# Loading x two batches per transfer, and moving the uneven share of the DMA engines from the first load to the first store

## Chip, cores, metric

One NeuronCore of a Trainium2 chip. The metric is the time of one execution on the device in microseconds (us). A kernel's time is the median of its runs; the profile is of one execution, and its span (first to last instruction) is about 1.8 us shorter than the time of the same run. PE is the TensorE matmul engine, DVE the VectorE, ACT the ScalarE; PSUM is the memory that PE writes its results to. The "pool queue" holds the transfers that GpSimd issues. A "packet" is one contiguous piece that one DMA engine moves.

## The reference

```python
x:      (32, 512, 1024) float32
weight: (32, 1024, 768) float32
np.matmul(x, weight).astype(np.float32)     # (32, 512, 768)
```

Each batch reads 2 MB of x and 3 MB of weight and writes 1.5 MB. There is no reuse between batches, so 32 batches have to move about 208 MiB.

## The kernel before

Loads go through the pool queue, which casts to bf16 on the way. PE transposes x (two bf16 as one float32 word), DVE copies the transposed words out of PSUM, PE multiplies, ACT and DVE move the result to `out_sb`, and the pool queue stores it. Near the end, stores are held back and sent by the sync engine.

```python
x_pool = ctx.enter_context(tc.tile_pool(name="x", bufs=5))     # w 4, xT 8, out 7
x_view = x.rearrange("b (mi mo) k -> b mi mo k", mi=P)         # partition mi: 4 rows, 16 KB
def load_x(b):
    xs[b] = x_pool.tile([P, MT, K], BF16, name="x_sb")
    nc.gpsimd.dma_start(out=xs[b], in_=x_view[b])
def transpose(b, mt):
    pt = tpsum.tile([P, JT, P], F32, name="pt")
    pairs = xs[b].bitcast(F32)
    for j in range(JT):
        nc.tensor.transpose(pt[:, j, :], pairs[:, mt, j::JT], ident)
    xT = xT_pool.tile([P, JT, P, 2], BF16, name="xT")
    nc.vector.tensor_copy(...)                                  # contiguous
    return xT
# ... first x: three quarters in one transfer, the last quarter in 18 small ones
nc.sync.dma_start(x_first[:, :MT - 1], x_view[0, :, :MT - 1])
at = 0
for few, times in ((4, 2), (5, 1), (6, 1)):
    for _ in range(times):
        for first in range(at, at + 4):
            rows = slice(first, at + 4 * few, 4)
            nc.sync.dma_start(x_first[rows, MT - 1], x_view[0, rows, MT - 1])
        at += 4 * few
# ... (two more)
for b in range(B):
    if b + AHEAD + 1 < B: load_x(b + AHEAD + 1)                 # AHEAD = 3
    if b + AHEAD < B:     load_w(b + AHEAD)
    # ... store of batch b - 1 on the pool queue, then the batch's compute
```

The Trainium skill (DMA: Bandwidth & Descriptors, "Why a DMA increments its semaphore by 16 and not by 1") says that the number of engines of a transfer is the largest one up to 16 that divides the outermost sizes of both its sides (here the partitions), and that the sync engine's transfers take the lowest-numbered. By that, a transfer over 4, 5 or 6 partitions does not use all 16 DMA engines, and the small transfers make a skew: more bytes for engines 0 to 3, fewer for the rest. The trace's packets carry no engine number.

Of the kernel before, what the change touches and what calls it, by code (L numbers as in the profile page):

```python
# [8 lines left out]
F32 = mybir.dt.float32  # L9
BF16 = mybir.dt.bfloat16  # L10


@with_exitstack
def kernel(
    ctx: ExitStack,
    tc: tile.TileContext,
    x: bass.AP,
    weight: bass.AP,
    out: bass.AP,
):  # L20
    nc = tc.nc
    B, M, K = x.shape
    _, _, N = weight.shape
    P = 128
    MT = M // P
    KT = K // P
    JT = KT // 2
    N2 = 2 * N
    CHUNKED = {B - 4: (4, 4), B - 3: (4, 4), B - 2: (4, 4), B - 1: (4, 2, 2)}
    AHEAD = 3  # L30
    LATE = 4
    HELD = 3

    const = ctx.enter_context(tc.tile_pool(name="const", bufs=1))
    first_pool = ctx.enter_context(tc.tile_pool(name="first", bufs=1))
    w_pool = ctx.enter_context(tc.tile_pool(name="w", bufs=4))
    x_pool = ctx.enter_context(tc.tile_pool(name="x", bufs=5))
    xT_pool = ctx.enter_context(tc.tile_pool(name="xT", bufs=8))
    out_pool = ctx.enter_context(tc.tile_pool(name="out", bufs=7))
    tpsum = ctx.enter_context(tc.tile_pool(name="tpsum", bufs=2, space=bass.MemoryType.PSUM))  # L40
    mpsum = ctx.enter_context(tc.tile_pool(name="mpsum", bufs=2, space=bass.MemoryType.PSUM))



    w_view = weight.rearrange("b (ki ko) n -> b ki ko n", ki=P)
    x_view = x.rearrange("b (mi mo) k -> b mi mo k", mi=P)
    out_view = out.rearrange("b (mi mo) n -> b mi (mo n)", mi=P)

    xs, ws, outs = {}, {}, {}

    def banks():
        return [mpsum.tile([P, 512], F32, name=f"pm{i}") for i in range(3)]

    def load_x(b):
        xs[b] = x_pool.tile([P, MT, K], BF16, name="x_sb")
        nc.gpsimd.dma_start(out=xs[b], in_=x_view[b])  # L56

    def load_w(b):
        ws[b] = w_pool.tile([P, KT, N], BF16, name="w_sb")
        at = 0  # L60
        for n in CHUNKED.get(b, (KT,)):
            nc.gpsimd.dma_start(out=ws[b][:, at:at + n, :], in_=w_view[b, :, at:at + n, :])  # L62
            at += n

    def transpose(b, mt):

        pt = tpsum.tile([P, JT, P], F32, name="pt")
        pairs = xs[b].bitcast(F32)
        for j in range(JT):
            nc.tensor.transpose(pt[:, j, :], pairs[:, mt, j::JT], ident)  # L70
        xT = xT_pool.tile([P, JT, P, 2], BF16, name="xT")
        nc.vector.tensor_copy(  # L72
            xT.rearrange("p j m r -> p (j m r)"), pt.bitcast(BF16).rearrange("p j m -> p (j m)")
        )
        return xT

    def transpose_first(mt):

        xT = xT_pool.tile([P, JT, P, 2], BF16, name="xT")
        for h in range(2):  # L80
            pt = tpsum.tile([P, JT, P], F32, name="pt")
            for i in range(JT):
                nc.tensor.transpose(pt[:, i, :], x_first[:, mt, JT * h + i::KT], ident)  # L83
            nc.vector.tensor_copy(  # L84
                xT[:, 2 * h:2 * h + 2].rearrange("p j m r -> p j r m"),
                pt.rearrange("p (j r) m -> p j r m", r=2),
            )
        return xT



    SPLITS = (
        ((0, 0, 0, 512), (1, 0, 512, N - 512)),
        ((1, N - 512, 0, 1024 - N), (2, 0, 1024 - N, N2 - 1024)),
    )

    def matmuls(pm, half, xT, b, kos, together):
        for ko in kos:
            for i, (bank, at, off, size) in enumerate(SPLITS[half]):
                shares = half == 1 and i == 0  # L100
                nc.tensor.matmul(  # L101
                    pm[bank][:, at:at + size],
                    xT[:, ko // 2, :, ko % 2],
                    ws[b][:, ko, off:off + size],
                    start=(ko == 0 and not (together and shares)),
                    stop=(ko == KT - 1),
                    skip_group_check=together,
                )

    def evacuate(b, pair, pm):  # L110
        o = outs[b][:, pair * N2:(pair + 1) * N2]
        nc.scalar.copy(o[:, 0:512], pm[0])  # L112
        nc.vector.tensor_copy(o[:, 512:1024], pm[1])  # L113
        nc.scalar.copy(o[:, 1024:N2], pm[2])  # L114

    with tc.manual_schedule():
        x_first = first_pool.tile([P, MT, K], F32)

        nc.sync.dma_start(x_first[:, :MT - 1], x_view[0, :, :MT - 1])
        at = 0  # L120
        for few, times in ((4, 2), (5, 1), (6, 1)):
            for _ in range(times):
                for first in range(at, at + 4):
                    rows = slice(first, at + 4 * few, 4)
                    nc.sync.dma_start(x_first[rows, MT - 1], x_view[0, rows, MT - 1])
                at += 4 * few
        for rows in (slice(at, 80), slice(80, P)):
            nc.sync.dma_start(x_first[rows, MT - 1], x_view[0, rows, MT - 1])
        load_w(0)
        ident = const.tile([P, P], F32)  # L130
        make_identity(nc, ident)
        for b in range(1, AHEAD):
            load_x(b)
            load_w(b)
        load_x(AHEAD)

        pending = []
        for b in range(B):
            if b + AHEAD + 1 < B:
                load_x(b + AHEAD + 1)  # L140
            if b + AHEAD < B:
                load_w(b + AHEAD)
            if b <= B - LATE:
                if b > 0:
                    pending.append(b - 1)
                if b + AHEAD < B - HELD or b == B - LATE:
                    for at in pending:
                        nc.gpsimd.dma_start(out=out_view[at], in_=outs[at])  # L148
                    pending = []
            if b == B - 1:  # L150
                halves = [slice(pair * N2, (pair + 1) * N2) for pair in range(2)]
                nc.sync.dma_start(out_view[b - 1, :, halves[0]], outs[b - 1][:, halves[0]])
                for late in range(B - LATE, B - 2):
                    nc.sync.dma_start(out_view[late], outs[late])
                nc.sync.dma_start(out_view[b - 1, :, halves[1]], outs[b - 1][:, halves[1]])
            outs[b] = out_pool.tile([P, MT * N], F32, name="out_sb")
            if b not in CHUNKED:
                turn = transpose if b else lambda _, mt: transpose_first(mt)
                xT = {mt: turn(b, mt) for mt in (0, 1)}
                for pair in range(2):  # L160
                    pm = banks()
                    for half in range(2):
                        if pair == 0:
                            matmuls(pm, half, xT[half], b, range(KT), False)
                            xT[2 + half] = turn(b, 2 + half)
                        else:
                            matmuls(pm, half, xT[2 + half], b, range(KT), False)
                    evacuate(b, pair, pm)
                continue
            xT = {0: transpose(b, 0)}  # L170
            pms = [banks() for _ in range(2)]
            at = 0
            for n in CHUNKED[b]:
                last = at + n == KT
                for mt in range(MT):
                    if mt + 1 not in xT and mt + 1 < MT:
                        xT[mt + 1] = transpose(b, mt + 1)
                    matmuls(pms[mt // 2], mt % 2, xT[mt], b, range(at, at + n), True)
                    if last and mt % 2 == 1:
                        pair = mt // 2  # L180
                        evacuate(b, pair, pms[pair])
                        if b == B - 1:
                            nc.sync.dma_start(out_view[b, :, halves[pair]], outs[b][:, halves[pair]])
                at += n
# [30 lines left out]
```

## Time and profile before

516.93 us, the median of the runs of the first measurement. The run that left the profile took 517.03.

From the page of the kernel before: the busy time of each engine, then rows of the 40 slices (each digit is tenths of a slice busy), then the DMA queues with packets, MB and share of 16 engines' span, and the traffic with HBM.

```profile
PE 419.6 (81%) x2576; PEld 275.7 (54%) x2576; DVE 129.8 (25%) x196; ACT 76.2 (15%) x129; POOL 51.7 (10%) x102
...
PE   0039999999999988798978879977898978989980
...
DMA  8999999999999999999999999999999999999996
...
q0 software_dynamic: 13824, 126.88, 96.7%
q1 hardware_dynamic: 1232, 8.39, 4.1%
...
HBM read 167.77 MB, written 50.33 MB: 423 GB/s over the span
```

The DMA row is 9 in every slice but the first and the last. PE is idle for its first two slices. From the same page, two groups (line, operation, output and input, count, then busy us and mean ns of one, then idle time before them and what ended it), and what the chain that ended last is made of:

```profile
L101 PE MATMUL pm<-w_sb,xT 128*128 128x256 bf16 (+1 forms) x2048 | 364.7, 336 | 47.9 <-DMA w_sb<-in_weight_dram 44.0
L72 DVE COPY xT<-pt 128x1024 bf16<-128x1024 bf16 x124 | 82.8, 689 | 203.0 <-PE pt L70 203.0
...
DMA 69%; PE 25%; DVE 2%; issue 1%; ACT 0%; POOLq 0%
```

The chain's pieces at its start and its end (start us, length us, what):

```profile
0.74 9.28 DMA x_first<-in_x_dram
...
10.04 10.89 DMA x_first<-in_x_dram
...
20.95 12.60 DMA x_first<-in_x_dram
...
33.64 3.89 PE pt L83 x16
...
501.22 0.58 ACT out_sb L114
```

The first x needs three rounds of transfers and PE starts at 33.6 us. It catches up by 127 us, and from then on waits for w. The pool queue's issues in the steady part, from the timeline, show the pace of one batch (198.85 - 183.03 us here, 15.8 us):

```profile
183.03 0.53 POOL L56 DMA_DIRECT2D x_sb<-in_x_dram  x1 [6.65 <-DMA w_sb<-in_weight_dram]
186.72 0.53 POOL L62 DMA_DIRECT2D w_sb<-in_weight_dram  x1 [3.16 <-DMA out_dram<-out_sb]
191.63 0.54 POOL L148 DMA_DIRECT2D out_dram<-out_sb  x1 [4.38 <-DVE xT L72]
198.85 0.53 POOL L56 DMA_DIRECT2D x_sb<-in_x_dram  x1 [6.69 <-DMA w_sb<-in_weight_dram]
```

### The profile page before, as it was taken

Reading aid. Unit: us, or ns where it says so; the run is one execution under the profiler, and the core shown is the slowest. Engines: PE = TensorE matmul, PEld = TensorE weight load, DVE = VectorE, ACT = ScalarE, POOL = GpSimd, SP = SyncE. Lnnn points to the kernel's source line nnn. Section 1 sums busy time; section 2 is a strip of 40 time slices with the busy share of each in tenths; the row PEclk is TensorE's granted clock in tenths of the full one; section 3 lists DMA queues with packets and bytes.
Section 4 is the critical chain, followed back from the end, with each engine's and each line's share of the span. In section 5 each row is a group of like instructions: output and inputs, shape, how many; then the busy total and the mean of one; then the engine's idle time right before and its main releaser. Section 6 shows DMA issues by size and latency. Waiting matters only on the chain.

```text
span 515.2 us, 6001 instructions
## 1 busy us (share of the span) xinstructions
PE 419.6 (81%) x2576; PEld 275.7 (54%) x2576; DVE 129.8 (25%) x196; ACT 76.2 (15%) x129; POOL 51.7 (10%) x102
## 2 busy tenths in 40 slices
PE   0039999999999988798978879977898978989980
PEld 0026666666666655465645545654564645656650
DVE  0023333333333313133122231322331313332320
ACT  0001111111111101011111111110110111111110
POOL 3000111111000110100101001100111010111000
PEclk9999999999999989799988997998997989999995
DMA  8999999999999999999999999999999999999996
GB/s 233 223 225 220 209 278 277 260 238 276 274 276 267 237 269 276 275 272 245 254 276 275 276 254 243 273 278 275 266 239 265 276 276 274 240 253 213 291 430 272
DMA packets 15081, 135.64 MB, mean 263 GB/s; under 512 B 1744, under 2 KB 1744, under 8 KB 3536
## 3 DMA queue, kind: packets, MB, share of 16 engines
q0 software_dynamic: 13824, 126.88, 96.7%
q1 hardware_dynamic: 1232, 8.39, 4.1%
q8 instruction: 20, 0.33, 0.2%
q14 instruction: 5, 0.04, 0.0%
HBM read 167.77 MB, written 50.33 MB: 423 GB/s over the span
## 4 chain that ended last, share of the span: by engine, by line
DMA 69%; PE 25%; DVE 2%; issue 1%; ACT 0%; POOLq 0%
DMA w_sb<-in_weight_dram 31%; PE pm L101 22%; DMA out_dram<-out_sb 16%; DMA x_sb<-in_x_dram 15%; DMA x_first<-in_x_dram 6%; PE pt L70 2%; PE pt L83 1%; DVE out_sb L113 1%; DVE xT L72 1%; ACT out_sb L112 0%; ACT out_sb L114 0%; POOLq L62 0%; POOLq L148 0%; POOLq L56 0%
## 5 line engine op out<-in xcount | busy, mean ns | idle before, releaser
L101 PE MATMUL pm<-w_sb,xT 128*128 128x256 bf16 (+1 forms) x2048 | 364.7, 336 | 47.9 <-DMA w_sb<-in_weight_dram 44.0
L101 PEld LDWEIGHTS <-xT 128*128 128x128 bf16 x2048 | 203.3, 100 | 184.6 <-issue 50.5
L72 DVE COPY xT<-pt 128x1024 bf16<-128x1024 bf16 x124 | 82.8, 689 | 203.0 <-PE pt L70 203.0
L112 ACT COPY out_sb<-pm 128x512 f32<-128x512 f32 x64 | 37.5, 585 | 286.7 <-PE pm L101 286.7
L70 PEld LDWEIGHTS pt<-ident,x_sb 128*128 128x128 f32 x496 | 72.9, 206 | 6.3 <-issue 1.3
L113 DVE COPY out_sb<-pm 128x512 f32<-128x512 f32 x64 | 44.0, 687 | 128.1 <-PE pm L101 128.1
L70 PE MATMUL pt<-ident,x_sb 128*128 128x128 f32 x496 | 75.4, 286 | 0.0
L114 ACT COPY out_sb<-pm 128x512 f32<-128x512 f32 x64 | 37.5, 586 | 138.2 <-PE pm L101 138.0
L62 POOL DMA_DIRECT2D w_sb<-in_weight_dram x37 | 19.8, 534 | 154.9 <-PE pm L101 74.6
L56 POOL DMA_DIRECT2D x_sb<-in_x_dram x31 | 16.5, 532 | 173.4 <-DMA w_sb<-in_weight_dram 129.4
L83 PE MATMUL pt<-ident,x_first 128*128 128x128 f32 x32 | 6.0, 350 | 33.6 <-DMA x_first<-in_x_dram 33.6
L148 POOL DMA_DIRECT2D out_dram<-out_sb x28 | 15.0, 536 | 93.2 <-DMA x_sb<-in_x_dram 55.9
L83 PEld LDWEIGHTS pt<-ident,x_first 128*128 128x128 f32 x32 | 5.0, 204 | 34.3 <-issue 33.6
L84 DVE CAST xT<-pt 128x512 bf16<-128x512 f32 x8 | 5.6, 726 | 40.7 <-PE pt L83 40.5
L112 ACT ACT_TABLE_LOAD x1 | 1.3, 1283 | 0.7 <-PEq L199 0.7
masks.py:199 POOL TENSOR_SCALAR_AFFINE_SELECT ident<-ident 128x128 f32<-128x128 f32 x1 | 0.3, 287 | 0.1
masks.py:197 POOL MEMSET ident<- 128x128 f32 x1 | 0.2, 223 | 0.0
L199 POOL MEMSET const-float32-0.0<- 128x1 f32 x1 | 0.1, 98 | 0.2 <-issue 0.2
L199 POOL MEMSET const-bfloat16-1.0<- 128x1 bf16 x1 | 0.1, 101 | 0.0
L199 POOL MEMSET const-uint8-127<- 128x1 uint8 x1 | 0.1, 101 | 0.0
L199 POOL MEMSET const-float32-1.0<- 128x1 f32 x1 | 0.1, 98 | 0.0
## 6 DMA issues: line engine op xcount, KB each, us to landing
w_sb<-in_weight_dram POOLq DMA_DIRECT2D x28, 1536.0 KB, 43.2
out_dram<-out_sb POOLq DMA_DIRECT2D x28, 1536.0 KB, 42.0
x_sb<-in_x_dram POOLq DMA_DIRECT2D x31, 1024.0 KB, 39.6
w_sb<-in_weight_dram POOLq DMA_DIRECT2D x7, 768.0 KB, 31.9
out_dram<-out_sb SPq DMA_DIRECT2D x4, 768.0 KB
out_dram<-out_sb SPq DMA_DIRECT2D x2, 1536.0 KB
x_first<-in_x_dram SPq DMA_DIRECT2D x1, 1536.0 KB
w_sb<-in_weight_dram POOLq DMA_DIRECT2D x2, 384.0 KB, 28.6
```

The lines of the kernel that those rows point to most:

```text
L56: nc.gpsimd.dma_start(out=xs[b], in_=x_view[b])
L62: nc.gpsimd.dma_start(out=ws[b][:, at:at + n, :], in_=w_view[b, :, at:at + n, :])
L70: nc.tensor.transpose(pt[:, j, :], pairs[:, mt, j::JT], ident)
L72: nc.vector.tensor_copy(xT.rearrange("p j m r -> p (j m r)"), pt.bitcast(BF16).rearrange("p j m -> p (j m)"))
L83: nc.tensor.transpose(pt[:, i, :], x_first[:, mt, JT * h + i::KT], ident)
L84: nc.vector.tensor_copy(xT[:, 2 * h:2 * h + 2].rearrange("p j m r -> p j r m"), pt.rearrange("p (j r) m -> p j r m", r=2),)
L101: nc.tensor.matmul(pm[bank][:, at:at + size], xT[:, ko // 2, :, ko % 2], ws[b][:, ko, off:off + size], start=(ko == 0 and not (together an ...
L112: nc.scalar.copy(o[:, 0:512], pm[0])
L113: nc.vector.tensor_copy(o[:, 512:1024], pm[1])
L114: nc.scalar.copy(o[:, 1024:N2], pm[2])
L148: nc.gpsimd.dma_start(out=out_view[at], in_=outs[at])
L199: nc = _bacc.Bacc("TRN2", target_bir_lowering=False, num_devices=1)
```

## The change

The intent: fewer and longer DMA packets for x, an earlier start of PE, and the skew of the engines in a place where nobody waits for it. Its core, with cuts:

```diff
-    x_pool = ctx.enter_context(tc.tile_pool(name="x", bufs=5))
-    xT_pool = ctx.enter_context(tc.tile_pool(name="xT", bufs=8))
+    x_pool = ctx.enter_context(tc.tile_pool(name="x", bufs=3))
+    xT_pool = ctx.enter_context(tc.tile_pool(name="xT", bufs=6))
+    pair_view = x[1:B - 1].rearrange("(p r) (mi mo) k -> p (r mi) mo k", r=2, mo=2 * MT)
 ...
+    def load_pair(b):
+        xs[b] = x_pool.tile([P, 2 * MT, K], BF16, name="x_sb")
+        nc.gpsimd.dma_start(out=xs[b], in_=pair_view[b // 2])
 ...
+    def transpose_pair(b, mt):
+        both = xT_pool.tile([P, 2, JT, P // 2, 2, 2], BF16, name="xT")
+        for half in range(2):
+            nc.vector.tensor_copy(
+                both[:, :, :, :, half, :].rearrange("p b j i r -> p j b i r"),
+                words(b, mt + MT * half).rearrange("p j (b i r) -> p j b i r", b=2, r=2),
+            )
 ...
+    def store(b):
+        cols = MT * N
+        if b == SKEWED:                         # SKEWED = 0
+            cols -= 512
+            for first in range(0, 120, 20):
+                for at in range(first, first + 4):
+                    rows = slice(at, first + 20, 4)
+                    nc.sync.dma_start(out_view[b, rows, cols:], outs[b][rows, cols:])
+            nc.sync.dma_start(out_view[b, 120:, cols:], outs[b][120:, cols:])
+        nc.gpsimd.dma_start(out=out_view[b, :, :cols], in_=outs[b][:, :cols])
 ...
-        x_first = first_pool.tile([P, MT, K], F32)
-        ... 19 transfers of x_first
+        x_first = x_pool.tile([P, MT, K], F32, name="x_sb")
+        nc.sync.dma_start(x_first, x_view[0])
 ...
-            if b + AHEAD + 1 < B:
-                load_x(b + AHEAD + 1)
+            if b % 2 and b + AHEAD + 1 < B:
+                ... load_last() for batch 31, else
+                    load_pair(b + AHEAD + 1)
 ...
+                if b % 2:
+                    for mt in range(MT):
+                        ready[b, mt], ready[b + 1, mt] = transpose_pair(b, mt)
```

A partition now holds eight consecutive rows of one batch of the pair (32 KB). The transposes of both batches come in one burst at the first of them.

More of the change, by code (lines that the diff above doesn't have):

```diff
@@ L32 @@
     HELD = 3
+    SKEWED = 0
     const = ctx.enter_context(tc.tile_pool(name="const", bufs=1))
-    first_pool = ctx.enter_context(tc.tile_pool(name="first", bufs=1))
     w_pool = ctx.enter_context(tc.tile_pool(name="w", bufs=4))
-    x_pool = ctx.enter_context(tc.tile_pool(name="x", bufs=5))
-    xT_pool = ctx.enter_context(tc.tile_pool(name="xT", bufs=8))
+    x_pool = ctx.enter_context(tc.tile_pool(name="x", bufs=3))
+    xT_pool = ctx.enter_context(tc.tile_pool(name="xT", bufs=6))
     out_pool = ctx.enter_context(tc.tile_pool(name="out", bufs=7))
@@ L52, in banks, with load_last @@
         return [mpsum.tile([P, 512], F32, name=f"pm{i}") for i in range(3)]
-    def load_x(b):
-        xs[b] = x_pool.tile([P, MT, K], BF16, name="x_sb")
-        nc.gpsimd.dma_start(out=xs[b], in_=x_view[b])
+    def load_pair(b):
+        xs[b] = x_pool.tile([P, 2 * MT, K], BF16, name="x_sb")
+        nc.gpsimd.dma_start(out=xs[b], in_=pair_view[b // 2])
+    def load_last():
+        xs[B - 1] = x_pool.tile([P, MT, K], BF16, name="x_sb")
+        nc.gpsimd.dma_start(out=xs[B - 1], in_=x_view[B - 1])
     def load_w(b):
@@ L63, in load_w, with words @@
             at += n
-    def transpose(b, mt):
+    def words(b, mo):
         pt = tpsum.tile([P, JT, P], F32, name="pt")
@@ L69, in transpose, with transpose_last @@
         for j in range(JT):
-            nc.tensor.transpose(pt[:, j, :], pairs[:, mt, j::JT], ident)
+            nc.tensor.transpose(pt[:, j, :], pairs[:, mo, j::JT], ident)
+        return pt.bitcast(BF16)
+    def transpose_pair(b, mt):
[5 more added lines that the diff above has]
+            )
+        return [both[:, r].rearrange("p j i h r -> p j (i h) r") for r in range(2)]
+    def transpose_last(mt):
         xT = xT_pool.tile([P, JT, P, 2], BF16, name="xT")
         nc.vector.tensor_copy(
-            xT.rearrange("p j m r -> p (j m r)"), pt.bitcast(BF16).rearrange("p j m -> p (j m)")
+            xT.rearrange("p j m r -> p (j m r)"), words(B - 1, mt).rearrange("p j m -> p (j m)")
         )
@@ L114, in evacuate @@
         nc.scalar.copy(o[:, 1024:N2], pm[2])
-    with tc.manual_schedule():
-        x_first = first_pool.tile([P, MT, K], F32)
-        nc.sync.dma_start(x_first[:, :MT - 1], x_view[0, :, :MT - 1])
-        at = 0
-        for few, times in ((4, 2), (5, 1), (6, 1)):
-            for _ in range(times):
-                for first in range(at, at + 4):
-                    rows = slice(first, at + 4 * few, 4)
-                    nc.sync.dma_start(x_first[rows, MT - 1], x_view[0, rows, MT - 1])
-                at += 4 * few
-        for rows in (slice(at, 80), slice(80, P)):
-            nc.sync.dma_start(x_first[rows, MT - 1], x_view[0, rows, MT - 1])
+    def store(b):
[8 more added lines that the diff above has]
+        nc.gpsimd.dma_start(out=out_view[b, :, :cols], in_=outs[b][:, :cols])
+    with tc.manual_schedule():
+        x_first = x_pool.tile([P, MT, K], F32, name="x_sb")
+        nc.sync.dma_start(x_first, x_view[0])
         load_w(0)
@@ L131 @@
         make_identity(nc, ident)
-        for b in range(1, AHEAD):
-            load_x(b)
-            load_w(b)
-        load_x(AHEAD)
+        load_pair(1)
+        load_w(1)
+        load_w(2)
+        load_pair(3)
+        ready = {}
         pending = []
         for b in range(B):
-            if b + AHEAD + 1 < B:
-                load_x(b + AHEAD + 1)
+            if b % 2 and b + AHEAD + 1 < B:
+                if b + AHEAD + 1 == B - 1:
+                    load_last()
+                else:
+                    load_pair(b + AHEAD + 1)
             if b + AHEAD < B:
@@ L147 @@
                     for at in pending:
-                        nc.gpsimd.dma_start(out=out_view[at], in_=outs[at])
+                        store(at)
                     pending = []
@@ L156 @@
             outs[b] = out_pool.tile([P, MT * N], F32, name="out_sb")
+            if b == 0:
+                xT = {mt: transpose_first(mt) for mt in range(MT)}
+            elif b == B - 1:
+                xT = {mt: transpose_last(mt) for mt in range(MT)}
+            else:
+                if b % 2:
+                    for mt in range(MT):
+                        ready[b, mt], ready[b + 1, mt] = transpose_pair(b, mt)
+                xT = {mt: ready.pop((b, mt)) for mt in range(MT)}
             if b not in CHUNKED:
-                turn = transpose if b else lambda _, mt: transpose_first(mt)
-                xT = {mt: turn(b, mt) for mt in (0, 1)}
                 for pair in range(2):
@@ L162 @@
                     for half in range(2):
-                        if pair == 0:
-                            matmuls(pm, half, xT[half], b, range(KT), False)
-                            xT[2 + half] = turn(b, 2 + half)
-                        else:
-                            matmuls(pm, half, xT[2 + half], b, range(KT), False)
+                        matmuls(pm, half, xT[2 * pair + half], b, range(KT), False)
                     evacuate(b, pair, pm)
                 continue
-            xT = {0: transpose(b, 0)}
             pms = [banks() for _ in range(2)]
@@ L175 @@
                 for mt in range(MT):
-                    if mt + 1 not in xT and mt + 1 < MT:
-                        xT[mt + 1] = transpose(b, mt + 1)
                     matmuls(pms[mt // 2], mt % 2, xT[mt], b, range(at, at + n), True)
```

## The prediction

> **What bounds the kernel now.** The DMA engines. In the page's 40 slices the DMA row is 9 everywhere except the first (8) and the last (6); the three queues take about 101% of 16 engines' span. PE is busy 81%, and the list of waits has it waiting 44.0 us for w_sb. The chain of waits is 69% DMA. In the timeline, from 130 to 400 us the pool queue issues one batch every 15.8 us; from 50 to 127 us, where PE catches up after its start at 33.6 us, a batch takes it 12.8 us. PE has 3 us to spare per batch; the time is DMA work plus its two ends.
>
> **What a transfer costs.** From the trace's packets, start to next start on an engine: a 16 KB read of x 606 ns, a 24 KB read of w 907 ns, a 12 KB read 455 ns: 0.0368 ns per byte and only some 3.4 ns per packet besides. Recorded lengths overlap by 19 ns. The Trainium skill (DMA: Bandwidth & Descriptors, "Bandwidth") says to batch to 1 MiB or more; these are 1 to 1.5 MB with 40 us queued, so that overhead is hidden already.
>
> **What the change does.**
> 1. Thirty x loads of 8 packets per engine become fifteen with packets twice as long: 120 packets fewer per engine, 120 x 3.4 ns = 0.4 us. On the critical path.
> 2. First x is one transfer. The chain shows three rounds of x_first (9.3 + 10.9 + 12.6 us); now it should land at 12 to 16 us and PE start there. Off the critical path: DMA was full.
> 3. The skew moves. Before, engines 0-3 got 20 rows of 4 KB where most others got 3 (168 ns each: 2.9 us more). Now engines 0-4 get 24 rows of 2 KB (my estimate 80 ns each: 1.9 us more). The last engine's data ends at 513.1 us, the mean engine's near 511.2, so 1.9 us of the span is imbalance; it can change by a microsecond either way.
> 4. All eight transposed groups of a pair come in one burst before its matmuls, with two PSUM buffers, and the copies write 4-byte pieces 8 bytes apart. If they keep 689 ns, a burst holds PE 5 to 6 us per pair; at one element per cycle (my estimate 1.22 us) 8 to 9 us. A batch then takes PE 12.9 to 14.5 us, still under 15.8. In the tail PE ends at 501 to 505 us; the last stores are issued now 9 us before DMA runs dry, so that is just covered.
>
> **Predicted:** 516.0 us, 514.6 to 517.2 with 8 chances in 10. Faster by over 2%: 0.01; within 2%: 0.97; slower by over 2%: 0.02.
>
> **What would show it.** Step 1: queue 0's packets fall by 15 x 128 + 15 x 16 = 2160 to 11664. Step 2: PE's first transpose before 17 us. Step 3: the DMA row's last slice, 6 before; fuller if the engines end closer together. Step 4: the mean of the DVE copies into xT, 0.69 or about 1.2 us; DMA slices still 9 throughout.
>
> **What would make it wrong.** Copies slower than 1.5 us would make PE the bound (over 16 us per batch). DMA idle in the last 40 us because PE ends after 509 us. A real per-packet overhead of 22 ns, as recorded lengths suggest: 514 us. A worse balance of engines: 518 us.

## The result

The first six runs gave 515.46 us in the median (514.88 to 517.72) against 516.93. The ratio is 0.9982 with a 95% interval of 0.9959 to 1.0006: the same within 2%, and not clearly different from 1. A ratio here is not quite the ratio of the medians. With two repeats (below) there are 17 runs, with a median of 516.14 us.

What I had not expected is the spread: 514.88 to 517.84 us, where the kernel before stays within 0.16 us.

The profile after is that of a long run (517.72 us). From its page, the rows that answer to those of before:

```profile
PE 440.0 (85%) x2576; PEld 279.6 (54%) x2576; DVE 129.9 (25%) x196; ACT 76.2 (15%) x129; POOL 43.8 (8%) x87
...
PE   0999969979799697996979979898797988999992
...
DMA  8999999999999999999999999999999999999996
...
q0 software_dynamic: 11664, 126.62, 96.2%
q1 hardware_dynamic: 1264, 8.65, 4.2%
```

PE starts in the second slice, queue 0 has 11664 packets as predicted, and the DMA row is the same digit for digit. The two groups and the make-up of the chain, from the same page:

```profile
L121 PE MATMUL pm<-w_sb,xT 128*128 128x256 bf16 (+1 forms) x2048 | 358.9, 339 | 43.3 <-DMA w_sb<-in_weight_dram 43.3
L84 DVE COPY xT<-pt 128x1024 bf16<-128x1024 bf16 x120 | 77.4, 687 | 11.0 <-PE pt L77 11.0
...
PE 64%; DMA 21%; DVE 7%; another core or an unknown queue 6%; issue 1%; ACT 0%
```

The copies still take 687 ns (689 before). The chain is now mostly PE, which looks as if the bound had moved. It has not: PE spends 43.3 us waiting for w, and the DMA row is full. In the steady part PE's compute of a batch and the release of its w buffer alternate with transfers, and the chain picks whichever ended last at each step. ("another core or an unknown queue" stands for waits whose releaser the profile did not find; there is one core.)

The chain's start and end, and the pool queue's issues in the steady part:

```profile
0.74 11.39 DMA x_sb<-in_x_dram
...
12.27 3.88 PE pt L103 x16
...
506.29 0.58 ACT out_sb L134
```

```profile
175.48 0.53 POOL L59 DMA_DIRECT2D x_sb<-in_x_dram  x1 [2.83 <-DMA out_dram<-out_sb]
184.80 0.53 POOL L69 DMA_DIRECT2D w_sb<-in_weight_dram  x1 [8.79 <-PE pm L121]
187.13 0.54 POOL L146 DMA_DIRECT2D out_dram<-out_sb  x1 [1.80 <-DMA out_dram<-out_sb]
200.87 0.53 POOL L69 DMA_DIRECT2D w_sb<-in_weight_dram  x1 [13.20 <-PE pm L121]
204.16 0.54 POOL L146 DMA_DIRECT2D out_dram<-out_sb  x1 [2.76 <-DMA w_sb<-in_weight_dram]
207.53 0.53 POOL L59 DMA_DIRECT2D x_sb<-in_x_dram  x1 [2.83 <-DMA out_dram<-out_sb]
```

The first x lands at 12.1 us and PE starts 21.4 us sooner (12.27 against 33.64). Nothing of that reaches the end, because DMA was busy from the second slice on in both kernels. Two batches take 32.05 us here (207.53 - 175.48), against 31.6 before. Over eight pairs it is 256.1 us (from the issue at 143.44 us to that at 399.55), where the profile of a shorter run (after_again, below) has 253.0 us (143.50 to 396.51) and 16 batches of the kernel before 253.4 us (151.47 to 404.89). So the long run loses time in the steady part.

Where? The trace lists every DMA packet with its start and length. In the kernel before, a packet of a given size nearly always has the same length: 925 or 926 ns for a 24 KB read of w. In the profile after, some reads of w take longer, mostly 970 to 1310 ns and in one case 1852 ns. Which packets follow one another on an engine is inferred, from starts that fall 19 ns before the end of an earlier load. The slowed reads come in clusters: the last one to three of the eight w packets of an engine, when the engines are about to go over to a store, or when some have already gone over. I counted the loads on the pool queue between 60 and 485 us that lasted over 20 ns longer than usual for their size, and summed what they lasted too long, divided by the 16 engines. The kernel before has 22 of them; the changed kernel, in this run, 159.

Adding up all packets, each with the usual time from start to start for its size instead of its recorded length, gives the work of a mean engine without slowed reads: 505.6 us before and 505.1 us after. That half microsecond is about the gain that I had predicted for the packets. The slowed reads in this run add 1.8 us per engine (0.24 us before) and more than eat it.

### The profile page after: what moved, and what is told of

Its sections match the earlier page's. It is cut to its first block, busy times and chain, and to the rows that moved or that the text cites. A ratio compares the mean times of both kernels' runs of the same rounds, so it can differ in the third digit from the quotient of the medians.

```text
span 515.9 us, 5853 instructions
## 1 busy us (share of the span) xinstructions
PE 440.0 (85%) x2576; PEld 279.6 (54%) x2576; DVE 129.9 (25%) x196; ACT 76.2 (15%) x129; POOL 43.8 (8%) x87
## 3 DMA queue, kind: packets, MB, share of 16 engines
q0 software_dynamic: 11664, 126.62, 96.2%
## 4 chain that ended last, share of the span: by engine, by line
PE 64%; DMA 21%; DVE 7%; another core or an unknown queue 6%; issue 1%; ACT 0%
PE pm L121 56%; DMA w_sb<-in_weight_dram 19%; PE pt L77 6%; DVE xT L84 4%; DMA x_sb<-in_x_dram 2%; DVE out_sb L133 2%; PE pt L103 1%; DVE xT L104 0%; DVE xT L92 0%; ACT out_sb L134 0%
## 5 line engine op out<-in xcount | busy, mean ns | idle before, releaser
L121 PE MATMUL pm<-w_sb,xT 128*128 128x256 bf16 (+1 forms) x2048 | 358.9, 339 | 43.3 <-DMA w_sb<-in_weight_dram 43.3
L121 PEld LDWEIGHTS <-xT 128*128 128x128 bf16 x2048 | 206.8, 101 | 190.8 <-DMA w_sb<-in_weight_dram 47.9
L77 PE MATMUL pt<-ident,x_sb 128*128 128x128 f32 x496 | 79.8, 302 | 10.5 <-DVE xT L84 10.2
L77 PEld LDWEIGHTS pt<-ident,x_sb 128*128 128x128 f32 x496 | 69.3, 209 | 21.5 <-DVE xT L84 18.7
L84 DVE COPY xT<-pt 128x1024 bf16<-128x1024 bf16 x120 | 77.4, 687 | 11.0 <-PE pt L77 11.0
L103 PE MATMUL pt<-ident,x_sb 128*128 128x128 f32 x32 | 6.7, 362 | 12.5 <-DMA x_sb<-in_x_dram 12.3
L103 PEld LDWEIGHTS pt<-ident,x_sb 128*128 128x128 f32 x32 | 5.1, 205 | 13.9 <-issue 12.2
L59 POOL DMA_DIRECT2D x_sb<-in_x_dram x15 | 8.0, 533 | 45.0 <-DMA out_dram<-out_sb 30.6
L92 DVE COPY xT<-pt 128x1024 bf16<-128x1024 bf16 x4 | 2.6, 686 | 0.2 <-PE pt L77 0.2
L63 POOL DMA_DIRECT2D x_sb<-in_x_dram x1 | 0.5, 528 | 6.7 <-DMA w_sb<-in_weight_dram 6.7
```

Of the source, the lines that this page charges most:

```text
L59: nc.gpsimd.dma_start(out=xs[b], in_=pair_view[b // 2])
L77: nc.tensor.transpose(pt[:, j, :], pairs[:, mo, j::JT], ident)
L84: nc.vector.tensor_copy(both[:, :, :, :, half, :].rearrange("p b j i r -> p j b i r"), words(b, mt + MT * half).rearrange("p j (b i r) -> ...
L92: nc.vector.tensor_copy(xT.rearrange("p j m r -> p (j m r)"), words(B - 1, mt).rearrange("p j m -> p (j m)"))
L103: nc.tensor.transpose(pt[:, i, :], x_first[:, mt, JT * h + i::KT], ident)
L121: nc.tensor.matmul(pm[bank][:, at:at + size], xT[:, ko // 2, :, ko % 2], ws[b][:, ko, off:off + size], start=(ko == 0 and not (together an ...
```

## The experiments

Twelve runs followed: the changed kernel twice more and ten variants; all gave correct results. They fell on four chips, and the kernel before, run beside each, is at 516.90 to 516.93 in the median on every one. The changed kernel itself stood beside others only on chip 9 (with pair_no_skew, pair_old_skew and single_new_skew) and on chip 11 (with order_and_tail and order_tail_less_skew). First, the changed kernel unaltered, twice more.

### after_again and after_third: no edit

> The changed kernel unaltered. Its six runs so far fall at 514.9 (three), 516.0, 517.6 and 517.7 us, where the kernel before stays within 0.1 us. Theory A (luck of the run: in some executions reads of w next to stores are slowed on some engines, as the profiled slow execution shows with 151 slowed w packets): 514.9 to 517.7 us again, and if this profile falls in a 514.9 us execution it shows far fewer than 151 slowed w packets and engines ending closer together. Theory B (a fixed, balanced time with noise of the first chip): all runs within 0.2 us of 514.9.

> The changed kernel once more, on the same chip as the two others, for a fair comparison and for its spread: 514.9 to 517.7 us, median 515.2 to 516. A profile with many slowed packets of w goes with a long run, one with few with a short one.

Measured: 515.86 us in the median (515.00 to 516.46), and 516.91 us (515.20 to 517.84). The second median lies above the 515.2 to 516 expected. The spread comes back within each chip (1.5 us and 2.6 us); theory B fell. Whether the chip moves the median of this kernel is not tested. The count of slowed loads was 65 in the profiled run of 515.61 us, 159 in that of 517.72 us and 214 in that of 517.15 us. So few go with a short run, but the count does not rank the two long ones. In the run of 517.72 us the last data packet ends 7.3 us after what the packets of a mean engine add up to, slowed reads included and instruction fetches left out (an estimate from the packets); in the run of 517.15 us it is 6.2 us, in that of 515.61 us 6.1 us. So in the longest run some engine ends later than the slowed reads of a mean engine account for. Which engines were hit, the trace does not say.

### pair_no_skew, pair_old_skew, single_new_skew, single_no_skew: two ways to load x, three skews

```diff
# pair_no_skew: after with
-    SKEWED = 0
+    SKEWED = -1
# pair_old_skew: the same, and the first x (still in a pair buffer) by the 19 transfers of before
-        nc.sync.dma_start(x_first, x_view[0])
+        nc.sync.dma_start(x_first[:, :MT - 1], x_view[0, :, :MT - 1])
+        ... 18 small ones
# single_no_skew: before with the first x in one transfer
-        nc.sync.dma_start(x_first[:, :MT - 1], x_view[0, :, :MT - 1])
-        ... 18 small ones
+        nc.sync.dma_start(x_first, x_view[0])
# single_new_skew: the same, and store(b) of the change for the pool queue's stores
```

> The changed kernel with the first store whole: no engine is given extra rows. My estimate from the ends of the engines: the five engines that had 24 rows of 2 KB end 1.3 us earlier, the others 0.6 us later; so 515.5 us where the changed kernel's fast runs give 514.9, if a late engine is among the others; 514 us if the late ones are among the five. Theory C: spread between runs as in the changed kernel.

> Pair loads, but the first x by its old 18 small row transfers and the first store whole. PE starts near 33 us again. Theory A (packets saved are worth 3.4 ns each, the rest is balance of the engines): the kernel before less 0.4 to 0.5 us, 516.4 us. Theory B (22 ns per packet): 514.2 us. Theory C (the spread between runs comes from the pair loads themselves): runs spread by over 1 us here too; if it comes from the moved skew or the early start of PE, they stay within 0.2 us.

> x of one batch per transfer as before, with the first x in one transfer and the first store skewed in five-row transfers. Theory A: balance alone; within 1 us of the kernel before (516 to 517.5 us), and 0.4 to 0.5 us slower than the changed kernel's fast runs if nothing else differs. If the whole gain of 2 us (514.9) is the skew's and the early start's, it appears here: 515.0 to 515.3 us. Theory C: no spread between runs.

> x of one batch per transfer, the first x in one transfer, no engine given extra rows. Completes the table of two ways to load x by three skews. Theory A (small independent parts): pairs are worth 0.1 to 0.5 us, so about 516.7 us beside the 516.35 us of pairs without skew, and the new skew is worth 0.3 to 0.5 us on top of either. Theory B (the skew is what mattered): over 517.5 us. Spread between runs below 0.6 us as in the other kernels with single loads.

Measured, median (lowest to highest) in us:

| x loads | no skew | old skew | new skew |
|---|---|---|---|
| one batch | 516.98 (516.74 to 517.44) | 516.93 (516.86 to 517.02), the kernel before | 516.41 (516.04 to 516.58) |
| pairs | 516.35 (516.19 to 518.00) | 516.80 (516.54 to 519.66) | 516.14 (514.88 to 517.84), the change |

Pairs are 0.13 to 0.63 us faster in each column, and the new skew 0.2 to 0.6 us faster than none in each row. The old skew is worth nothing with single loads and costs 0.45 us with pairs; but wherever it stands, PE also starts late (33.6 us, and 40.5 us in pair_old_skew, against 12.2 to 12.5), so this table does not part the two. The change's cell pools all its 17 runs, of more than one chip; on chip 9 alone, with the other runs of its row and single_new_skew, it is 515.86. The parts are small and of the size of the spread, so only the signs that repeat should be believed. Nothing supports a 22 ns packet, which would have given 514.2 us for pair_old_skew. No gain is seen from the early start of PE: single_no_skew has it (12.31 us; its PE row is 9 in the second slice) and is at 516.98. But it lost the old skew with the same edit, so strictly the two could cancel. Where all x come singly the spread is 0.2 to 0.7 us, where they come in pairs 1.8 to 3.1 us. So within this table theory C held: the spread comes with the pairs. (The orders tried below show that it need not.) Missed were pair_no_skew, which the ends of the engines had put at 514 or 515.5 us, pair_old_skew, put at 516.4, and single_no_skew, put at 516.7 with a spread below 0.6.

### w_four_packets: the cost of a packet

```diff
-        ws[b] = w_pool.tile([P, KT, N], BF16, name="w_sb")
+        ws[b] = w_pool.tile([P, KT // 2, N2 + 32], BF16, name="w_sb")
-            nc.gpsimd.dma_start(out=ws[b][:, at:at + n, :], in_=w_view[b, :, at:at + n, :])
+            nc.gpsimd.dma_start(out=ws[b][:, at // 2:(at + n) // 2, :N2],
+                in_=w_view[b, :, at:at + n, :].rearrange("p (q two) n -> p q (two n)", two=2))
```

> The kernel before with rows of w padded in its buffer after every two of eight, so that each partition's 24 KB read of w goes as four packets in the same transfer, with the same bytes. Per engine 8 x (28 x 3 + 3 x 2 + 1) = 728 more packets. Theory A (3.4 ns per packet from start to start): 2.5 us more, 519.4 us. Theory B (22 ns per packet, as recorded lengths suggest): 16 us more, 533 us. If packets were free: 516.9 us.

Measured: 519.75 us (519.64 to 519.78), 2.85 us over the kernel before beside it (516.90), with 728 packets more per engine (the trace has 16384 packets of w where it had 4736; the difference over 16 is 728). That is 3.9 ns per packet. So 120 packets fewer are worth 0.47 us. (PE started at 22.2 us in this run, not at 33.6; if that saved anything, a packet costs more.) The DMA queue of this run, from its page:

```profile
q0 software_dynamic: 25472, 126.88, 99.3%
q1 hardware_dynamic: 1232, 8.39, 4.1%
```

The recorded time of queue 0 went from 96.7% of 515.2 us to 99.3% of 517.9 us, 16 us more per engine, while the kernel took 2.85 us more, and the two queues add up to 103%. Recorded packet lengths overlap (the next packet of an engine starts 19 ns before a load ends), and so their fixed part must not be read as a cost.

### stores_by_two and pair_before_stores: another order on the pool queue

The kernel before has x, w, store; the change has pair, w, store, w, store. These keep everything of the change but the order: pair, w, w, store, store, and w, w, pair, store, store.

```diff
# stores_by_two
-                if b + AHEAD < B - HELD or b == B - LATE:
+                if (b % 2 == 0 or b == B - HELD - LATE) and b + AHEAD < B - HELD or b == B - LATE:
# pair_before_stores: the same, and instead of load_pair ahead of load_w at odd b
             if b + AHEAD < B:
                 load_w(b + AHEAD)
+            if b % 2 == 0 and 0 < b and b + AHEAD < B:
+                ... load_last() for batch 31, else load_pair(b + AHEAD)
```

> The changed kernel with the pool queue's order per two batches pair, w, w, store, store instead of pair, w, store, w, store: no w is queued behind a store any more, one w still ahead of one. Theory A (the last packets of w are slowed on some engines where a w is queued behind a store, which the kernel before never does): under 30 w packets slowed by over 20 ns between 60 and 485 us (151 and 57 in the two profiles of the changed kernel, 8 before), runs within 0.3 us of each other, median 514.9 us or less. Theory B (it is w ahead of a store, or something else): 50 or more slowed, spread over 1 us again.

> Order w, w, pair, store, store: no w is ahead of a store, one is behind one. Theory A (w behind a store is what slows): 50 or more slowed packets of w, spread of 1 us or more. Theory B (w ahead of a store): under 30 slowed, spread within 0.3 us, median 514.9 us or less. If both orders have many slowed packets, adjacency is not the cause.

Measured: 515.25 us (514.71 to 515.37) and 514.99 us (514.47 to 515.58), 0.3 to 0.4% faster than the kernel before, which counts as the same at 2% but is clear of noise (ratios 0.9966, 0.9953 to 0.9978, and 0.9962, 0.9950 to 0.9975). Slowed loads in the profiles: 46 and 48, of them 39 and 21 reads of w, against 65 to 214 with the changed kernel's order. Neither theory held as it was put: both orders help, neither brought the count down to the 22 of the kernel before, and the spreads are 0.66 and 1.11 us, not 0.3. The changed kernel did not run on this chip; the order of the next section is compared with it directly.

The table at the end of the experiments shows one thing more. Where the pair of x stands right ahead of the stores (pair_before_stores, and order_and_tail below), 27 and 30 reads of x are slowed; where a w stands there, 6 to 9 reads of a pair that comes in one transfer. Chained by their starts, and leaving out the loads that lie beside an instruction fetch, most of the slowed reads are the last or last but one of their transfer on an engine with a store next, whether they read w or x. So it is the load right ahead of a store that is hit. What the two orders share is half as many changes between loads and stores per two batches; but the kernel before has as many changes as the changed kernel and hardly any trouble, so that isn't the whole cause either.

The second order also made PE late at the end, because it loads the last x last. Busy time by stretch for pair_before_stores (us, then the engines, then the granted clock, the DMA share and GB/s):

```profile
499.00:503.00 4.00, 3.95 (x26) 2.34 (x25) 0.00 (x0) 0.00 (x0) 0.00 (x0) 1.00 1.00 419
503.00:507.00 4.00, 4.00 (x27) 2.44 (x26) 0.61 (x1) 1.04 (x2) 0.00 (x0) 1.00 0.85 359
507.00:511.00 4.00, 0.76 (x5) 0.29 (x3) 0.77 (x2) 1.26 (x3) 0.00 (x0) 0.90 0.81 332
```

From 503 us on the DMA share falls to 0.85 while PE still computes: the last stores are not there yet.

### order_and_tail and order_tail_less_skew: that order with the changed kernel's end

```diff
# order_and_tail: pair_before_stores with
-            if b % 2 == 0 and 0 < b and b + AHEAD < B:
+            if b % 2 == 0 and 0 < b and b + AHEAD < B - HELD:
# and the changed kernel's lines again, ahead of load_w, for the last pair and the last x
+            if b % 2 and B - HELD <= b + AHEAD + 1 < B:
+                ... load_last() for batch 31, else load_pair(b + AHEAD + 1)
# order_tail_less_skew: the same with
-            cols -= 512
+            cols -= 384
```

> The order w, w, pair, store, store of the run before, but the last pair and the last x are loaded where the changed kernel loads them, so that PE ends near 503 us instead of 508 and the engines do not run dry at 503 to 509 us (23 engine-us, 1.4 us per engine, in the run with that order). If those 1.4 us are the time's: 513.6 to 514.4 us, faster than the changed kernel and than the 514.99 us of that order. If the imbalance of the engines sets the end all the same: 514.5 to 515.3 us.

> The same with 384 instead of 512 columns of the first store in the five-row transfers. In the run with stores by two, five engines seem to end 1 us after the others. If those are the five with the extra rows, this ends 0.2 to 0.4 us sooner than with 512 columns; if they are others, 0.1 to 0.3 us later.

Measured: order_and_tail 514.61 us (514.45 to 514.81), ratio 0.9956 (0.9944 to 0.9968). It is the fastest kernel, ahead of both the kernel before (by 2.3 us) and the changed kernel on the same chip in the same rounds (516.91), and its spread is 0.36 us. The same stretches show DMA full until PE is done:

```profile
499.00:503.00 4.00, 3.05 (x19) 1.63 (x17) 1.38 (x2) 2.30 (x4) 0.00 (x0) 1.00 1.03 438
503.00:507.00 4.00, 0.00 (x0) 0.00 (x0) 0.00 (x0) 0.00 (x0) 0.00 (x0) 0.84 0.99 416
507.00:511.00 4.00, 0.00 (x0) 0.00 (x0) 0.00 (x0) 0.00 (x0) 0.00 (x0) 0.50 0.79 332
```

The time fell by 0.38 us only (from 514.99, measured on another chip), in the range that was put on imbalance. The idle stretch is mended (0.99 against 0.85 from 503 to 507 us), but the engines end at different moments now, between about 508.5 and 511.6 us where all of pair_before_stores' end within 511.8 to 512.0; that takes most of it back. Less skew gave 515.01 us (514.61 to 515.38), 0.40 us later: no gain by less of it was seen, and by its expectation the late engines are not those with the extra rows. The runs of the two overlap.

### pair_two_transfers: is it the long packets or the order?

```diff
-        nc.gpsimd.dma_start(out=xs[b], in_=pair_view[b // 2])
+        for part in (slice(0, MT), slice(MT, 2 * MT)):
+            nc.gpsimd.dma_start(out=xs[b][:, part], in_=pair_view[b // 2][:, part])
```

> The changed kernel, same order on the queue, but each pair of x comes in two transfers of 16 KB reads as before (half of every partition's rows each), so the packets are the size of the kernel before. Theory A (the order pair, w, store, w, store is what brings slowed packets of w and the spread between runs): over 50 slowed packets of w, runs spread by over 1 us, median 515.5 to 517 us. Theory B (the 32 KB reads bring them): under 30 slowed, spread within 0.5 us, 515 to 515.6 us, since 120 packets per engine more cost only 0.4 to 0.5 us.

Measured: 515.86 us (515.42 to 516.30), 92 slowed loads, 79 of them of w. The reads of x are as short as before the change and the slowed reads of w are still there, so they do not need the 32 KB packets. The spread, 0.88 us in five runs, lies between what the two theories said; the count and the median are theory A's.

The slowed loads, counted as above, in all profiles but that of w_four_packets, whose reads of w have another size:

```
kernel              slowed w / x   too long, us per engine   time of the profiled run, us
before                  12 / 10            0.24                 517.03
order_tail_less_skew    14 / 43            0.70                 514.61
order_and_tail          16 / 30            0.68                 514.61
pair_before_stores      21 / 27            0.56                 514.99
single_no_skew          30 / 15            0.64                 517.41
stores_by_two           39 /  7            0.62                 515.27
single_new_skew         56 / 13            0.71                 516.50
pair_no_skew            58 /  7            0.91                 516.19
after_again             59 /  6            1.18                 515.61
pair_old_skew           78 /  9            2.18                 519.66
pair_two_transfers      79 / 13            1.19                 516.30
after                  152 /  7            1.82                 517.72
after_third            208 /  7            2.38                 517.15
```

In the six profiles with the order pair, w, store, w, store the excess is 0.91 to 2.38 us per engine, in the seven others 0.24 to 0.71; but the changed kernel apart, each kernel has one profile. The order is not all: with x, w, store as in the kernel before, 12, 30 and 56 reads of w are slowed as only the first x and the skew differ.

The counts quoted in the expectations leave out the half-size loads of w near the end and differ by a few. Instruction fetches (20 packets of 16 KB in every profile) lengthen one or two loads each, which is most of the 22 in the kernel before.

## Why the prediction was right or wrong

The predicted time, 516.0 us with 514.6 to 517.2, holds: 515.46 in the first measurement, 516.14 over 17 runs. That the median falls so near the point is partly luck. The short runs gain 2 us, of which the steps forecast 0.4 us and left a microsecond either way open; the long runs lose it to slowed reads that no step has. Point by point:

1. **The packets: right.** 0.4 us was predicted from 3.4 ns per packet between starts. The direct measurement is 3.9 ns, so 0.47 us; pairs against single loads gave 0.13 to 0.63 us. No sign is seen that fifteen transfers fewer bring anything else. The Trainium skill (DMA: Bandwidth & Descriptors, "Anatomy of one DMA — SWDGE (gpsimd) path") fits one transfer by itself with 2.0 us plus its bytes; fifteen times 2.0 us would have been 30 us. With a full queue none of it shows here. What does agree is its figure for the fabric (section "Where 436 GB/s comes from"): 435.2 GB/s over 16 engines is 27.2 bytes per ns, and the slope of packet time against bytes in this trace, 0.0368 ns per byte, is 27.2 bytes per ns. The DMA engines run close to that rate here from end to end (423 GB/s over the whole span, from the page of the kernel before), which is why so little was to be had.
2. **The early start: right.** PE's first transpose came at 12.27 us (12 to 16 said), and in single_no_skew no gain came with it.
3. **The skew: right in kind.** "It can change by a microsecond either way": the new skew is 0.5 us faster than the old with single loads (516.41 against 516.93), and about 0.7 us with pairs (516.14 against 516.80), where the spread blurs it. In both rows PE's early start changes along with it.
4. **PE and DVE: right on the copies, slightly short at the end.** The copies took 687 ns, so they kept the 689 ns. The Trainium skill (VectorE: DVE Perf Modes, "Mode 2×_1P — pack two bf16 into one 32-bit read") asks for 16-bit data with step 1; runs of two elements, 8 bytes apart, agree with that: the copies are no slower than the contiguous ones. The burst held PE 5.7 us (88.38 to 94.05 us in the timeline). PE's end was put at 501 to 505 us "just covered"; in the three profiles the last copy after it starts at 503.1, 504.6 and 506.3 us.

What the prediction did not have is a step for the order on the pool queue. It took a read of w to last 907 ns from start to start whatever its neighbours were. With pair, w, store, w, store some reads of w last mostly 5 to 40% longer, one in the profile after twice as long, differently in each run, up to 2.4 us per engine. With this go the 4 of 17 runs above 517.2 us, and a mean gain over 17 runs of 0.7 us where the short runs gain 2; only three of the 17 were profiled. Shown: the slowed reads are there, without the long x packets too; they are the last reads ahead of a store, of w or of x; two other orders have fewer, and one of them, with the changed kernel's tail, has shorter and steadier times on the same chip in the same rounds (514.61 with a spread of 0.36 us, against 516.91 with 2.64). Not shown: why a read is slowed. All 16 engines in step, or certain addresses read beside certain addresses written, would both fit the clusters. The kernel before, with a store after every w, has only 7 slowed loads that do not lie beside an instruction fetch, and its skew alone is not the reason: pair_old_skew has that skew, and 78 slowed reads of w. That stays open.

## What to carry to other kernels

When DMA is full from end to end, count bytes first, then packets from start to start, not by their recorded lengths; merging transfers that were already a megabyte gained 0.1 to 0.6 us of 517 here. What is left is the order in which loads and stores follow each other on the queue and how evenly the engines end, so try two or three orders before finer things. And run a kernel several times: a spread that the old version did not have is itself a finding.

## What the Trainium skill lacked or had wrong

- DMA: Bandwidth & Descriptors gives about 10.5 ns per packet (section "Measured (HBM→SBUF, 128 partitions, SWDGE, issued from GpSimd)"): the floor of one small transfer shared out over its 64 packets on all engines. It must not be read as what a packet more costs in a full queue, which is 3.9 ns on each engine here (2.85 us for 728).
- No page says that recorded packet lengths overlap, by 19 ns for loads here, and so overstate what a packet costs: queue 0's recorded time rose by 16 us per engine in w_four_packets, and the kernel's by 2.85 us.
- No page says that the last loads ahead of a store on one queue can take longer, and by more in some orders of loads and stores than in others: 65 to 214 slowed loads in the six profiles with pair, w, store, w, store, against 22 in the kernel before, with a spread of 3.0 us between runs against 0.16 us.
